# A two-layer decoder trunk on one core: one subtraction, four products and one load change their engine

## Chip, core and metric

The kernel runs on one core of a Trainium2 chip. A core has five engines that run at the same time, each with its own queue of instructions, taken in order: TensorE (PE, matrix products), VectorE (DVE), ScalarE (ACT, functions by table, and copies), GpSimd (POOL) and SyncE (SP, which here only issues transfers). ScalarE can issue transfers as well. Transfers themselves are done by 16 DMA engines that all queues share. The metric is device microseconds for one execution of the whole program, the median of several runs.

## What is computed

The reference is a decoder trunk of two layers on 256 tokens of 1024 features, in float32. Layer 0 mixes tokens by a gated spatial unit (gMLP), layer 1 by an mLSTM; each layer then has a SwiGLU channel mixer and a gated embedding. The parts that the change touches are the first product of layer 0 and the mLSTM's cell and output:

```python
def gmlp_mixer(x, w_in, ...):
    z = jax.nn.gelu(x @ w_in)
    u, v = jnp.split(z, 2, axis=-1)
    ...

def mlstm_cell(q, k, v, i_pre, f_pre):          # 4 heads of 512, chunks of 128
    ...
        s = jnp.einsum('bhtd,bhsd->bhts', qb, kb) * jnp.exp(dmat - m_t[..., None])
        num = (jnp.einsum('bhts,bhsd->bhtd', s, vb) + ...)
        h = num / jnp.maximum(jnp.abs(den), jnp.exp(-m_t))[..., None]

def mlstm_mixer(x, ...):
    h = mlstm_cell(split_heads(q), split_heads(k), split_heads(v), i_pre, f_pre)
    h = layer_norm(h, norm_g).reshape(B, S, ML_INNER) + skip * xc
    return (h * jax.nn.silu(z)) @ w_out
```

With 256 tokens in two chunks the kernel forms the cell's chunks in closed form: for each head a matrix P of scores times decay (the text calls it P), then P·V, then a division and a normalisation per head.

## The kernel before

**Precision by two parts.** A float32 operand is kept as two float32r tiles: the high part is a rounded copy, the low part the difference. Three matmuls (high·high, low·high, high·low) replace one. The helper `split` (lines 151 to 153) makes both: the copy on ScalarE (`act.copy`), the subtraction on VectorE, or on the engine named in `sub`. Every weight tile of 128 x 1024 that arrives goes through it once, so line 153 is the line of nearly all copies and subtractions in the profile; they are told apart by tile names (`w` weights, `xs` x, `phi`/`plo` the two parts of P, `h` the down projection's input).

**Who sets the order.** The instructions of an engine are ordered by a planner that simulates the program with costs of its own and takes what is ready; the text of the kernel gives priorities. Inside `manual_schedule` (line 372 for ScalarE and VectorE at the start, line 859 for ScalarE during the gates) the order is that of the text. All weights come in the order of `weight_plan` through `ahead` (lines 170 to 204), which issues loads on SyncE's queue up to 8 tiles ahead and splits up to 4 tiles ahead; only 4 raw tiles exist, so a load waits for the subtraction that frees a raw tile.

**The start (lines 353 to 390).** TensorE runs eight warm-up matmuls on zeros. x comes transposed in four loads `xr[0..3]` of two 128-row blocks each. `xr[0]` is split in two: its first block is issued by ScalarE (line 363), its second by SyncE through the hook `second_x` (line 364), which `ahead` calls between the two halves of the first weight tile (lines 175 to 178). The first tiles come in halves of 512 columns. Lines 374 to 385 then split x's blocks and the weight halves in an order written by hand: for each block ScalarE copies the block's high part (L378), VectorE or ScalarE copies the weight half's (L380 or L382), and VectorE makes the low parts (L383, L384). TensorE's first matmuls are those of line 422, six for each block.

**The gates and P (lines 859 to 923).** For each of the four heads VectorE adds a mask (L909, tile `gm`), ScalarE takes three exponentials (L911 to L913, tile `e`), VectorE multiplies the scores by them (L917, tile `sc`), and `split` makes `phi` on ScalarE and `plo` on GpSimd (L920).

**P·V and the normalisation (`pv_block`, lines 930 to 967).** For each head TensorE multiplies `phi` and `plo` with V into two PSUM banks `num` (L937 to L939) and sums P's rows into `pd` (L943, L944). VectorE forms the denominator (L949 to L953), the statistics of `num` (L957, L958) and a variance (L961); GpSimd takes the reciprocal root (L962); VectorE finishes scale and shift (L963, L965); ScalarE writes the normalised head `hn` (L967), which frees the two banks. Between two heads TensorE has a block of z (`z_mm`).

**The down projection's input (`h_block`, lines 971 to 983).** For each head TensorE transposes `hn` (L976), VectorE applies the norm's gain and adds the skip (L980, tile `y`), multiplies with silu(z) (L981, tile `sz`), and `split` makes the two parts of `h`. Head 0's `h_block` is called after the third head's `pv_block` and z block, the other heads' during the down projection (`acc`, lines 992 to 1008), whose four PSUM banks are the ones that `num` used. The first three blocks of the projection are held until all are there, and added together (lines 1001 to 1006).

Of the kernel before, what the change touches and what calls it, by code (L numbers as in the profile page):

```python
# [12 lines left out]
ALU = mybir.AluOpType  # L13
# [51 lines left out]
def stationary(key):  # L65

    return key[0] in ("u", "xm") and len(key) == 2 or key[0] in ("g", "u", "z") and key[-1] >= 4


def paired(key):  # L70

    return key[0] in ("g", "u") and len(key) == 3 and key[-1] >= 4 or key[0] == "u" and len(key) == 2
# [61 lines left out]
def trunk(ctx, tc, a, out):  # L134
    nc = tc.nc
    pe, act, dve, pool, sp = nc.tensor, nc.scalar, nc.vector, nc.gpsimd, nc.sync
# [8 lines left out]
    def tl(tag, shape, dt=F32, name="t"):  # L145
        return sb.tile(shape, dt, tag=tag, name=name, bufs=BUFS[tag])
# [4 lines left out]
    def split(hi, lo, src, fast=False, sub=dve):  # L151

        return dve.tensor_copy(hi, src) if fast else act.copy(hi, src), sub.tensor_tensor(lo, src, hi.bitcast(F32), ALU.subtract)  # L153
# [7 lines left out]
    def issue_after(ops):  # L161

        stack = ExitStack()
        for op in ops:
            stack.enter_context(tc.issue_after(op.ins))
        return stack

    at = {"load": 0, "cast": 0, "use": 0}

    def ahead(loads, casts):  # L170
        while at["load"] < min(len(plan), at["use"] + loads):
            ap = plan[at["load"]][1]
            n = ap.shape[-1]
            t = tl("raw", [P, n], name="raw")
            for c in HALF if at["load"] < 3 else [slice(0, n)]:
                at["dma"] = sp.dma_start(t[:, c], ap[:, c])
                if at["load"] == 0 and c.start == 0:
                    second_x()
            raws[at["load"]] = t
            at["load"] += 1  # L180
        while at["cast"] < min(len(plan), at["use"] + casts):
            i = at["cast"]
            key, raw = plan[i][0], raws.pop(i)
            n = raw.shape[-1]
            if key in WIDE:
                t = tl("b8", [P, 2, D], F32R, "w")
            else:


                first = ASIDE if stationary(key) and not paired(key) else 0  # L190
                step = D + ASIDE if paired(key) else D
                t = tl("w", [P, 2 * D + P], F32R, "w")[:, first:first + 2 * step]
                t = t.rearrange("p (i n) -> p i n", i=2)[:, :, :D]
            with issue_after(behind["cast"]):
                if key[0] == "bdv":

                    t = t.rearrange("p i n -> p (i n)")[:, :4 * 2 * GW].rearrange("p (j i n) -> p j i n", j=4, i=2)
                    split(t[:, :, 0, :P], t[:, :, 1, :P], raw.rearrange("p (j n) -> p j n", j=4))
                    f = 4 * key[1]
                    pool.tensor_copy(t[:, :, :, P:], wx[:, f:f + 4, :].rearrange("p j (i n) -> p j i n", i=2))  # L200
                for c in () if key[0] == "bdv" else HALF if i < 3 else [slice(0, n)]:
                    split(t[:, 0, c], t[:, 1, c], raw[:, c])
            wt[i] = t
            at["cast"] += 1
# [153 lines left out]
    xr = []  # L358
    for i in range(4):
        t = tl("m2", [P, 2, S], name="xr")  # L360
        if i == 0:

            act.dma_start(t[:, 0, :], a["xT"][i, :, 0, :])
            second_x = lambda: sp.dma_start(xr[0][:, 1, :], a["xT"][0, :, 1, :])
            xr.append(t)
        else:
            sp.dma_start(t, a["xT"][i])
            xr.append(t)
        ahead(1 + i, 0)
    make_identity(nc, ident)  # L370
    pool.memset(mhalf, -0.5)
    with tc.manual_schedule(engines={mybir.EngineType.Activation, mybir.EngineType.DVE}):

        for i in range(2):
            w, raw = tl("w", [P, 2 * D + P], F32R, "w")[:, :2 * D].rearrange("p (i n) -> p i n", i=2), raws.pop(i)
            for k, h in enumerate(HALF):
                c = 2 * i + k
# [9 lines left out]
    for i in range(2, 4):  # L387
        c = slice(2 * i, 2 * i + 2)
# [4 lines left out]
    for c in range(6):  # L393
# [20 lines left out]
        for kp in range(4):  # L414
            w = weight("v", c, kp)
            for kk in range(2):
                k = 2 * kp + kk
# [284 lines left out]
    def mlstm(embed1):  # L702
# [32 lines left out]
        sz = [tl("b8", [P, 8, S], name="sz") for _ in range(2)]  # L735
# [97 lines left out]
        for s in range(NI + 3):  # L833
            if s < NI:
                y = xm_block(s)
# [23 lines left out]
        with tc.manual_schedule(engines={mybir.EngineType.Activation}):  # L859
            gp = bank("A", [4, 2, S], "gp")  # L860

            def transpose_gates():
                for i in range(2):
                    for t in range(2):
                        pe.transpose(gp[:, i, TOK[t]], gacc[:, t, 4 * i:4 * i + 4], ident)


            tc.keep_in_program_order(act.preload_act_table_set("natural_log_exp_and_others"))
            z8 = z_mm(8, {3: transpose_gates})
            dve.tensor_scalar(fs, gp[:, 1, :], gbias[:, 1:2], None, ALU.add)  # L870
            dve.scalar_tensor_tensor(ex, fs, -1.0, fs, ALU.mult, ALU.min)
            act.activation(ex, ex, AF.Exp)
            act.activation(ex, ex, AF.Ln, bias=1.0)
            dve.scalar_tensor_tensor(fs, fs, 0.0, ex, ALU.min, ALU.subtract)
            dve.tensor_tensor_scan(ex, line, fs, 0.0, ALU.mult, ALU.add)
            dve.scalar_tensor_tensor(ai, gp[:, 0, :], gbias[:, 0:1], ex, ALU.add, ALU.subtract)
            dve.tensor_tensor_scan(G, ai, ai, 0.0, ALU.max, ALU.max)
            dve.tensor_tensor(ex, ex, G, ALU.add)
            Gs = [tl("s", [4, S], F32R, "G") for _ in range(2)]
            behind["cast"] = split(*Gs, G, fast=True)[1:]  # L880
            z_copy(*z8)
            z_copy(*z_mm(9))
            cp = bank("A", [P, 4, 4], "cp")

            def transpose_cols():
                for i, src in enumerate((ai, ex)):
                    for t in range(2):
                        pe.transpose(cp[:, 2 * i + t, :], src[:, TOK[t]], ident[:4, :4])

            gbs = []  # L890

            def broadcast_gates():

                gbs.extend(bank("A", [P, 2, 2, P], "gb") for _ in range(2))
                for h in range(NH):
                    for i in range(2):
                        pe.matmul(gbs[h // 2][:, h % 2], selH[:, h, :], Gs[i], start=i == 0, stop=i == 1)

            z = z_mm(10, {2: transpose_cols, 4: broadcast_gates})
            dve.tensor_copy(cols[:, 0:2, :], cp[:, 0:2, :])  # L900

            dve.tensor_scalar(cols[:, 2:4, :], cp[:, 2:4, :], -88.0, None, ALU.max)
            for h in range(NH):
                if h == 1:
                    z_copy(*z)
                    z = z_mm(11)
                gb = gbs[h // 2][:, h % 2]
                gm = tl("s", [P, 2, P], name="gm")
                dve.tensor_tensor(gm, gb, cmask.unsqueeze(1).to_broadcast([P, 2, P]), ALU.add)  # L909
                e = tl("m2", [P, 384], name="e")  # L910
                act.activation(e[:, 0:P], gm[:, 0, :], AF.Exp, bias=cols[:, 0, h:h + 1], scale=-1.0)  # L911
                act.activation(e[:, P:S], gb[:, 1, :], AF.Exp, bias=cols[:, 0, h:h + 1], scale=-1.0)
                act.activation(e[:, S:384], gm[:, 1, :], AF.Exp, bias=cols[:, 1, h:h + 1], scale=-1.0)  # L913
                if h == 1:
                    act.activation(cols[:, 2:4, :], cols[:, 2:4, :], AF.Exp, scale=-1.0)
                p = sc[h]
                dve.scalar_tensor_tensor(p, p, DH ** -0.5, e, ALU.mult, ALU.mult)  # L917
                hi = tl("h", [P, 384], F32R, "phi")
                lo = tl("h", [P, 384], F32R, "plo")
                split(hi, lo, p, sub=pool)  # L920
                ph.append((hi, lo))
            z_copy(*z)
            act.activation(sz[1][:, 0:4, :], sz[1][:, 0:4, :], AF.Silu)
# [47 lines left out]
        def h_block(h):  # L971
            for j in range(2):
                tp = bank("B", [P, 2, S], "tp")
                for i in range(2):
                    for t in range(2):
                        pe.transpose(tp[:, i, TOK[t]], hn[h][:, t, (2 * j + i) * P:(2 * j + i + 1) * P], ident)  # L976
                for i in range(2):
                    f = 4 * h + 2 * j + i
                    y = tl("s", [P, S], name="y")
                    dve.scalar_tensor_tensor(y, tp[:, i, :], par[:, f, 6:7], a1[f // 8][:, f % 8, :], ALU.mult, ALU.add)  # L980
                    dve.tensor_tensor(y, y, sz[f // 8][:, f % 8, :], ALU.mult)  # L981
                    hs[f] = tl("h", [P, 2, S], F32R, "h")
                    split(hs[f][:, 0, :], hs[f][:, 1, :], y)

# [119 lines left out]
```

## Time and profile before

| What | Value |
|---|---|
| median of 3 runs | 825.69 us (825.42 to 826.16) |
| profiled execution's own time | 825.63 us |
| its span in the profile | 823.9 us |
| data read from HBM | 153.67 MB, 188 GB/s over the span |
| granted TensorE clock | 1.0 throughout |

The profile shows one execution. A row of a timeline gives the start and the duration in us, the engine, the line, the operation, the output tile, the input tiles and their shapes, and in brackets the time for which the engine was idle before it and what ended that idleness. "PEld" is TensorE's loading of stationary operands, which overlaps its matmuls. In the list of waits a row reads: the engine and line that waited, the one that released it, then total us, number of waits, and the longest. Several instructions of a kind can be merged into one row with a count (x2, x3); its duration is then that of all of them. Rows that name line 153 and a tile group a helper's instructions by what they work on. In a row of a window stand its start and end, its length, the busy time and count of each engine, the granted clock, the mean busy share of the 16 DMA engines, and GB/s.

### The profile page before, as it was taken

The numbers are of one execution on the slowest core, as the hardware profiler recorded it, in microseconds if no ns is written. First come the engines' busy times: TensorE is split into PE (matmuls) and PEld (weight loads), VectorE is DVE, ScalarE is ACT, GpSimd is POOL, SyncE is SP. The second block draws the span as 40 slices with busy tenths as digits, with TensorE's granted clock in tenths as the row PEclk, the third lists the DMA queues.
The fourth block names the chain that finished last, engine by engine and source line by source line (L and its number), as shares of the span: only waits on it lengthen the run. The fifth ranks groups of instructions, "written<-read, shape, count | busy, mean of one in ns | idle before, by whom it ended". The sixth has DMA issues, their size and how long they took to land.

```text
span 823.9 us, 12407 instructions
## 1 busy us (share of the span) xinstructions
PE 816.9 (99%) x4520; PEld 708.0 (86%) x4520; DVE 614.3 (75%) x982; ACT 470.9 (57%) x820; POOL 149.6 (18%) x209
## 2 busy tenths in 40 slices
PE   9999999999999999999999999999999999999997
PEld 6888888888888888888889999988888888888886
DVE  6757998678956567586878998889885656776674
ACT  6656666565535556475256788776444555665522
POOL 1020643342000000700001677330000000000000
PEclk9999999999999999999999999999999999999999
DMA  8895447567176678677144355454626667886501
GB/s 287 283 337 182 153 159 225 179 194 243 67 260 202 192 225 281 201 229 252 38 146 156 135 162 161 146 177 147 215 90 224 196 199 228 269 264 212 179 1 51
DMA packets 44997, 155.52 MB, mean 189 GB/s; under 512 B 5256, under 2 KB 6024, under 8 KB 44936
## 3 DMA queue, kind: packets, MB, share of 16 engines
q1 hardware_dynamic: 44792, 154.60, 57.6%
q8 instruction: 35, 0.57, 0.3%
q14 instruction: 26, 0.21, 0.1%
q10 hardware_dynamic: 144, 0.13, 0.0%
HBM read 153.67 MB, written 1.05 MB: 188 GB/s over the span
## 4 chain that ended last, share of the span: by engine, by line
PE 96%; DVE 1%; ACT 1%; DMA 1%; issue 0%; POOL 0%; SPq 0%; DVEq 0%; ACTq 0%
PE acc L240 9%; PE acc L241 9%; PE acc L242 9%; PE pu L260 8%; PE pg L260 8%; PE ups L260 5%; PE pg L264 4%; PE pu L264 4%; PE ups L264 3%; PE vps L242 2%; PE vps L240 2%; PE vps L241 2%; PE xmps L245 2%; PE xmps L247 2%; PE xmps L246 2%; PE gate L289 2%
## 5 line engine op out<-in xcount | busy, mean ns | idle before, releaser
L153 DVE TENSOR_TENSOR w<-raw,w 128x1024 fp32r<-128x1024 f32 (+1 forms) x275 | 333.2, 1219 | 74.7 <-ACT w L153 73.1
L153 ACT CAST w<-raw 128x1024 fp32r<-128x1024 f32 (+1 forms) x275 | 284.9, 1046 | 120.6 <-PE acc L242 25.7
L240 PE MATMUL acc<-w,h 128*128 128x512 f32 x336 | 133.0, 396 | 0.2 <-ACT hn L967 0.2
L241 PE MATMUL acc<-w,h 128*128 128x512 f32 x336 | 131.3, 391 | 0.0
L242 PE MATMUL acc<-w,h 128*128 128x512 f32 x336 | 131.0, 390 | 0.0
L242 PEld LDWEIGHTS acc<-w,h 128*128 128x128 f32 x336 | 63.1, 188 | 13.9
L240 PEld LDWEIGHTS acc<-w,h 128*128 128x128 f32 x336 | 63.1, 188 | 12.1 <-ACT hn L967 0.6
L241 PEld LDWEIGHTS acc<-w,h 128*128 128x128 f32 x336 | 63.1, 188 | 11.2 <-DVE h L153 0.2
L260 PE MATMUL pg<-xs,w 128*128 128x512 f32 x288 | 71.6, 391 | 0.0
L260 PE MATMUL pu<-xs,w 128*128 128x512 f32 x288 | 71.5, 390 | 0.0
L260 PEld LDWEIGHTS pg<-xs,w 128*128 128x128 f32 x288 | 53.8, 188 | 11.0
L260 PEld LDWEIGHTS pu<-xs,w 128*128 128x128 f32 x288 | 53.8, 188 | 11.0
L319 POOL TENSOR_TENSOR rs<-ve,mhalf 128x1 f32<-128x1 f32 x8 | 7.6, 956 | 295.9 <-DVE ve L318 291.3
L271 ACT COPY s<-pg 128x256 f32<-128x256 f32 x36 | 13.4, 372 | 69.7 <-PE pg L264 69.7
L260 PE MATMUL ups<-xs,w 128*128 128x512 f32 x192 | 47.9, 391 | 0.0
L272 DVE TENSOR_TENSOR s<-s,pg 128x256 f32<-128x256 f32 x36 | 15.1, 421 | 42.8 <-ACT s L271 42.7
L260 PEld LDWEIGHTS ups<-xs,w 128*128 128x128 f32 x192 | 35.7, 188 | 7.2
L264 PEld LDWEIGHTS pg<-xs,w 128*128 128x128 f32 x288 | 38.9, 188 | 3.1
L264 PE MATMUL pg<-xs,w 128*128 128x256 f32 x288 | 39.5, 280 | 0.0
L264 PE MATMUL pu<-xs,w 128*128 128x256 f32 x288 | 39.4, 279 | 0.0
L264 PEld LDWEIGHTS pu<-xs,w 128*128 128x128 f32 x288 | 36.5, 188 | 0.3
L245 PE MATMUL xmps<-xs,w 128*128 128x256 f32 x128 | 36.3, 284 | 0.0
(252 smaller groups left out, 1635.7 us busy)
## 6 DMA issues: line engine op xcount, KB each, us to landing
raw<-in_ffn_g SPq DMA_DIRECT2D x44, 512.0 KB, 4.4
raw<-in_ffn_u SPq DMA_DIRECT2D x44, 512.0 KB, 4.6
raw<-in_ffn_d SPq DMA_DIRECT2D x44, 512.0 KB, 4.3
raw<-in_gm_u SPq DMA_DIRECT2D x24, 512.0 KB, 3.5
raw<-in_gm_wo SPq DMA_DIRECT2D x24, 512.0 KB, 3.4
raw<-in_gm_v SPq DMA_DIRECT2D x21, 512.0 KB, 5.2
raw<-in_ple_gate SPq DMA_DIRECT2D x16, 512.0 KB, 4.5
raw<-in_ml_z SPq DMA_DIRECT2D x16, 512.0 KB, 3.8
```

Source lines behind the costliest of these rows:

```text
L153: return dve.tensor_copy(hi, src) if fast else act.copy(hi, src), sub.tensor_tensor(lo, src, hi.bitcast(F32), ALU.subtract)
L240: pe.matmul(ps, lh, w[:, 0, c], start=start, stop=False)
L241: pe.matmul(ps, ll, w[:, 0, c], start=False, stop=False)
L242: pe.matmul(ps, lh, w[:, 1, c], start=False, stop=stop)
L245: pe.matmul(ps, w[:, 0, c], h, start=start, stop=False)
L246: pe.matmul(ps, w[:, 0, c], l, start=False, stop=False)
L247: pe.matmul(ps, w[:, 1, c], h, start=False, stop=stop)
L260: pe.matmul(ps, w[:, 0, k * P:(k + 1) * P], xs[:, k], start=k == 0, stop=False)
L264: pe.matmul(ps[:, 0], w[:, 1, k * P:(k + 1) * P], xh[:, k, :], start=False, stop=k == KD - 1)
L271: act.copy(o, ps[:, 1])
L272: dve.tensor_tensor(o, o, ps[:, 0], ALU.add)
L289: pe.matmul(ps, xl[:, k, TOK[t]], w[:, 0, c], start=False, stop=k == KD - 1)
```

## The change

Three places change. x's second block is issued by ScalarE right behind the first, and the hook between the halves of the first weight tile goes. The low part of P of head 0 is subtracted on VectorE; the other three heads' stay on GpSimd. The four products of head 0 with silu(z) go from VectorE to GpSimd; the other heads' stay on VectorE. What is computed is the same.

```diff
             for c in HALF if at["load"] < 3 else [slice(0, n)]:
                 at["dma"] = sp.dma_start(t[:, c], ap[:, c])
-                if at["load"] == 0 and c.start == 0:
-                    second_x()
...
         if i == 0:
-
-            act.dma_start(t[:, 0, :], a["xT"][i, :, 0, :])
-            second_x = lambda: sp.dma_start(xr[0][:, 1, :], a["xT"][0, :, 1, :])
+            for k in range(2):
+                act.dma_start(t[:, k, :], a["xT"][i, :, k, :])
             xr.append(t)
...
                 lo = tl("h", [P, 384], F32R, "plo")
-                split(hi, lo, p, sub=pool)
+
+                split(hi, lo, p, sub=pool if h else dve)
...
                     dve.scalar_tensor_tensor(y, tp[:, i, :], par[:, f, 6:7], a1[f // 8][:, f % 8, :], ALU.mult, ALU.add)
-                    dve.tensor_tensor(y, y, sz[f // 8][:, f % 8, :], ALU.mult)
+
+                    (dve if h else pool).tensor_tensor(y, y, sz[f // 8][:, f % 8, :], ALU.mult)
```

## The prediction

> **What bounds the kernel now.** I read the page first (busy shares), then TensorE's own waits, then the timelines around each wait.
>
> ```profile
> PE 816.9 (99%) x4520; PEld 708.0 (86%) x4520; DVE 614.3 (75%) x982; ACT 470.9 (57%) x820; POOL 149.6 (18%) x209
> ...
> PE warm L357 <- DVE warm L354: 1.2, 1, 1.2
> PE vps L422 <- ACT w L382: 0.6, 1, 0.6
> PE num L939 <- POOL plo L153: 0.5, 1, 0.5
> PE vps L422 <- ACT xs L378: 0.2, 1, 0.2
> PE acc L240 <- ACT hn L967: 0.2, 1, 0.2
> ...
> 818.46 1.12 PE L289 MATMUL gate<-w,xs 128*128 128x256 f32 x8
> ```
>
> The reader is to see that TensorE is busy for 816.9 of the 823.9 us span, and that the idle 7.0 us are almost listed: 1.2 before the first warm-up matmul, 0.2 + 0.6 in the first product of the kernel, 0.5 in the mLSTM's first P·V, 0.2 at the start of the down projection, and the tail after the last matmul (818.46 + 1.12 = 819.58, to 823.9: 4.3). The change takes no matmul away, so it can win only what stands in these waits. It touches three of them: 0.6, 0.5 and 0.2.
>
> **Part 1: x's second block on ScalarE's queue.** The chain of waits at the start:
>
> ```profile
> 1.24 0.42 SPq L364
> ...
> 1.71 4.98 DMA raw<-in_gm_v
> 6.72 0.63 ACT w L382
> ...
> 7.39 4.38 PE vps L422 x18
> ```
>
> ```profile
> 0.79 0.40 ACTq L363 DMA_DIRECT2D xr<-in_xT  x1
> ...
> 4.57 0.71 ACT L378 CAST xs<-xr 128x256 fp32r<-128x256 f32 x2 [2.06 <-DMA xr<-in_xT]
> ...
> 7.39 0.50 PE L422 MATMUL vps<-w,xs 128*128 128x512 f32 x1 [0.57 <-ACT w L382]
> ...
> 8.09 0.43 DVE L380 CAST w<-raw 128x512 fp32r<-128x512 f32 x1
> ...
> xr<-in_xT SPq DMA_DIRECT2D x1, 128.0 KB, 3.6
> ...
> 0.00:5.00 5.00, 3.60 (x8) 1.04 (x8) 0.93 (x3) 1.72 (x3) 2.57 (x14) 1.00 0.53 165
> 5.00:10.00 5.00, 4.41 (x17) 3.07 (x18) 3.97 (x9) 2.84 (x6) 0.00 (x0) 1.00 1.03 358
> ```
>
> SyncE's queue issues the first weight half, x's second block (1.24), then the second weight half (1.71). That half lands at 1.71 + 4.98 = 6.69, ScalarE casts it (0.63), and TensorE, which had finished the first block's six matmuls, has stood for 0.57. With the block on ScalarE's queue every later issue on SyncE moves up by 1.71 - 1.24 = 0.47. On ScalarE the second issue costs some 0.4 (the first one's duration) at a time when the engine next does something useful at 4.57, after an idle 2.06 behind its table load, so the issue is hidden; were that cover gone it would cost 0.4.
>
> What the earlier issue is worth is bounded: at best the whole 0.57, at worst nothing if transfers and not issues set the landing: the DMA share (next to last column of the two window rows) is 0.53 over the first 5 us, which holds the idle first two, and 1.03 over the next five, with the same bytes to move. Below nothing is rival C. Between these there is a second stop: the next block's weight is cast at 8.09 + 0.43 = 8.52, and it is used after six of the 18 matmuls (4.38 / 18 = 0.243 each), at 7.39 + 1.46 = 8.85. If that half lands no earlier, TensorE can move up by only 0.33. I take **-0.3**, the value with this nearest row behind it, and keep 0 and -0.57.
>
> **Part 2: head 0's low part on VectorE.** Around the 0.47 us stall:
>
> ```profile
> 533.81 0.74 DVE L909 TENSOR_TENSOR gm<-gb,cmask 128x256 f32<-128x256 f32 x2
> ...
> 533.91 0.51 ACT L153 CAST phi<-sc 128x384 fp32r<-128x384 f32 x1 [0.65 <-DVE sc L917]
> ...
> 534.47 1.20 DVE L153 TENSOR_TENSOR w<-raw,w 128x1024 fp32r<-128x1024 f32 x1
> ...
> 534.50 2.04 POOL L153 TENSOR_TENSOR plo<-sc,phi 128x384 fp32r<-128x384 f32 x1 [11.40 <-ACT phi L153]
> ...
> 535.60 1.36 DVE L917 SCALAR_TENSOR_TENSOR sc<-sc,e 128x384 f32<-128x384 f32 x1
> ...
> 536.60 0.50 PE L939 MATMUL num<-vn,plo 128*128 128x512 f32 x1 [0.47 <-POOL plo L153]
> ...
> 542.51 1.02 POOL L153 TENSOR_TENSOR plo<-sc,phi 128x384 fp32r<-128x384 f32 x1 [1.04 <-ACT phi L153]
> ...
> L153 DVE TENSOR_TENSOR xs<-xr,xs x2: 682/684/685, 10.3 to 12.1; 128x512 fp32r<-128x512 f32 x2
> ...
> L383 DVE TENSOR_TENSOR xs<-xr,xs x4: 419/420/426, 5.0 to 9.4; 128x256 fp32r<-128x256 f32 x4
> ```
>
> GpSimd began at 534.50 while VectorE was in a weight's low part to 535.67, and ended at 536.54; alone (542.51) the same subtraction takes 1.02. VectorE's next two-input instruction, which began at 535.60, took 1.36 and ended at 536.96. So the two engines take turns: each waited for the other's end. On VectorE the subtraction lies between the 0.42 of 256 columns and the 0.68 of 512: about 0.55. It can start when ScalarE's high part is there (534.42). VectorE is free at about 534.5, so it ends near 535.05 ahead of the 1.20 weight part, or near 536.2 behind it. TensorE wants it at 536.60 - 0.47 = 536.13. Ahead, the whole **-0.47** comes; behind, about -0.4. If VectorE waits for the high part before the next head's mask (L909 at 533.81), its 0.6 of waiting falls on heads 1 to 3, whose low parts are used one gate product and more later. The order on VectorE is a planner's, so either is possible; both are gains. In return VectorE's 1.36 shrinks towards 0.5, which pays for the added 0.55.
>
> **Part 3: head 0's products on GpSimd, and what is late next.** TensorE arriving 0.47 earlier meets the last of the waits, the bank that the fourth head's numerator leaves:
>
> ```profile
> 555.00 0.76 DVE L981 TENSOR_TENSOR y<-y,sz 128x256 f32<-128x256 f32 x2
> ...
> 553.74 0.69 POOL L962 TENSOR_TENSOR hrs<-hrs,mhalf 128x2 f32<-128x2 f32 x1 [5.60 <-DVE hrs L961]
> ...
> 556.46 1.01 ACT L153 CAST h<-y 128x256 fp32r<-128x256 f32 x3
> ...
> 558.25 0.15 DVE L949 SCALAR_TENSOR_TENSOR dn<-pd,cols 128x2 f32<-128x2 f32 x1
> ...
> 558.32 1.21 DVE L153 TENSOR_TENSOR w<-raw,w 128x1024 fp32r<-128x1024 f32 x1
> ...
> 560.15 0.48 PE L240 MATMUL acc<-w,h 128*128 128x512 f32 x1
> ...
> 560.92 1.29 DVE L957 BATCH_NORM_STATS2 hst<-num 128x6 f32<-128x512 f32 x2
> ...
> 564.51 1.45 ACT L967 ACTIVATE hn<-num,nb,hrs 128x512 f32<-128x512 f32 x2 [0.75 <-DVE nb L965]
> ...
> 565.35 0.50 PE L240 MATMUL acc<-w,h 128*128 128x512 f32 x1 [0.18 <-ACT hn L967]
> ...
> 556.33 0.25 PE L944 MATMUL pd<-ones_r,plo 128*128 128x2 f32 x1
> ...
> L153 POOL TENSOR_TENSOR vn<-vsum,vn 128x256 fp32r<-128x256 f32 x2 | 1.5, 740 | 0.3 <-ACT vn L153 0.2 <-ACT gsum L825 0.2
> ```
>
> TensorE finished the fourth head at 556.33 + 0.25 = 556.58, but VectorE took its denominators up only at 558.25 and its statistics at 560.92, and ScalarE normalised at 564.51. That chain is late because VectorE is full, not because TensorE is. If nothing else changed, the 0.47 would be lost here: the stall of 0.18 would read 0.65. The four products take 0.38 each on VectorE (0.76 for two), so moving them frees 1.5 us ahead of 558.25. That is more than the 0.65 needed, which is why I let both go: **-0.18** more.
>
> The products themselves cost 0.74 each on GpSimd, by its nearest row (also two inputs, 256 columns; the ends are VectorE's own 0.38 and the 1.02 of 384 columns); four take 3.0, from 554.4 when GpSimd ends the root of L962 to 557.4, or about 559 with waits for VectorE. Queued behind each on ScalarE is its cast of h, and behind that VectorE's low part. ScalarE was taking those casts from 556.46 only, after head 2's normalisation, and TensorE reads the first of them at 560.15 and the next ones 1.36 (six matmuls of 0.227) apart; a cover of 2 us or more. If it is gone, TensorE waits for the products directly. GpSimd's next duty, head 3's root near 563, is far behind.
>
> [...]
>
> **Sum**, on the profiled execution's own time of 825.63 (span 823.9 and 1.73 around it; the median of the three runs is 0.06 higher): -0.3 - 0.47 - 0.18 = -0.95, so 824.7.
>
> **Rivals.**
> A. *GpSimd's turns cost VectorE more than the products did.* All four turns on the chain: 4 x 0.74 = 2.96 locked, less 1.5 saved, and the fourth head's normalisation comes up to 1.44 later. The 0.47 goes into that wait and TensorE resumes at 565.35 + 1.44. With -0.3 from the start: +1.14, 826.8, slower than before. It decides from the point where VectorE loses more than 1.5 us to GpSimd's turns. For it: the 1.36 row, and a VectorE that is full here. [...] 0.08.
> B. *The stall only moves.* The products' results come late in VectorE's order, its low parts of h wait, and the denominators start where they did: 0.47 is lost at the bank, only -0.3 stays: 825.3. For it: the denominators stand behind three low parts in the timeline. 0.13.
> C. *x's second block lands late.* It lands at 1.24 + 3.6 = 4.84 now, and ScalarE casts it ahead of the weight half in an order written by hand. If it comes only with the half, at 6.69, the half's cast is 0.36 later (0.71 for two casts); this begins to cost past 6.36. +0.36 - 0.47 - 0.18 = -0.29: 825.3. Against: 1.5 us of room. 0.08.
> [...]
> D. *The first part does nothing*, transfers being the limit: -0.65, 825.0. For it: the share of 1.03. 0.17.
>
> **How the numbers follow.** Forecast 824.7: 0.50; A 0.08; B 0.13; C 0.08; D 0.17; 0.04 for an order of the planner that none of this covers. Best sum -0.57 - 0.47 - 0.18 = -1.22 gives 824.4; the runs lie 0.27 below and 0.47 above their median. The range 824.2 to 826.0 takes in all but A and the last. About 0.2% (1.65 us) is what a measurement of this kernel can tell from no change; below 824.04 nothing in the touched waits reaches, above 827.34 not even A. Faster 0.04, same 0.92, slower 0.04.
>
> **What would show it.** Right: the wait of TensorE on plo is gone from its list, the first head's plo stands on VectorE within 0.5 to 0.6 us, the wait on hn is gone, and the wait on L382 has shrunk to about 0.3. Part 1 is wrong if the weight half still lands at 6.7; C shows as the cast of x's second block starting after 6.3. B shows as a wait on hn of 0.6; A as one above 0.65, with two-input VectorE instructions near 1 us between 554 and 560. The forecast as a whole fails if TensorE shows a wait at a place not listed above.

## The result, and the profile after

| | before | changed |
|---|---|---|
| median, 11 executions each | 825.66 us (825.19 to 826.16) | 828.17 us (826.96 to 830.48) |
| ratio | | 1.0035, 95% interval 1.0027 to 1.0043 |
| profiled execution's own time | 825.63 us | 829.92 us |
| its span | 823.9 us | 828.2 us |

The forecast was 824.7. The kernel became 2.5 us slower. TensorE's list of waits in the profile of the changed kernel (lines here are two or three lower than before: L238 is the old L240, L965 the old L967, L935 the old L937):

```profile
PE acc L238 <- ACT hn L965: 2.2, 1, 2.2
...
PE num L935 <- ACT e L909: 1.0, 1, 1.0
PE vps L419 <- DVE w L377: 0.6, 1, 0.6
```

The wait for `plo` is gone, as intended. The wait for `hn` has grown from 0.2 to 2.2, and a wait of 1.0 stands where there was none. The page's first part says that this is not all:

```profile
PE 818.8 (99%) x4520; PEld 709.2 (86%) x4520; DVE 615.1 (74%) x979; ACT 470.8 (57%) x820; POOL 152.9 (18%) x212
```

TensorE has the same 4520 matmuls, and is idle for 828.2 - 818.8 = 9.4 us, 2.4 more than before; but it is also busy for 1.9 us longer than the 816.9 of before. Together that is the 4.3 by which this execution is longer. The 1.9 are a clock. The timeline of TensorE behind its longest wait:

```profile
567.34 0.50 PE L238 MATMUL acc<-w,h 128*128 128x512 f32 x1 [2.19 <-ACT hn L965]
567.67 0.57 PE L239 MATMUL acc<-w,h 128*128 128x512 f32 x1
...
570.60 0.63 PE L240 MATMUL acc<-w,h 128*128 128x512 f32 x1
...
571.31 0.39 PE L239 MATMUL acc<-w,h 128*128 128x512 f32 x1
```

and that stretch as a window (the clock is the third number from the end):

```profile
567.67:571.08 3.41, 3.41 (x10) 2.66 (x9) 3.11 (x8) 2.42 (x5) 0.00 (x0) 0.51 0.00 0
```

For 3.41 us the granted clock was half, and matmuls started every 0.43 us instead of every 0.23. The cost is about 3.41 x (1 - 0.51) = 1.7 us. Not every execution has it: of the eleven, five show a mean clock of 0.997 to 0.998 and took 829.23 to 830.48 (mean 829.68), six show 0.999 or 1.0 and took 826.96 to 828.17 (mean 827.63). So some 2.0 us of the loss are there always, and another 2.0 in about half of the executions.

**Where the waits come from.** First ScalarE before the change, around head 1's high part (`phi` at 537.00):

```profile
535.59 1.05 ACT L153 CAST w<-raw 128x1024 fp32r<-128x1024 f32 x1
537.00 0.51 ACT L153 CAST phi<-sc 128x384 fp32r<-128x384 f32 x1 [0.36 <-DVE sc L917]
...
538.27 1.03 ACT L153 CAST w<-raw 128x1024 fp32r<-128x1024 f32 x1
...
540.15 0.35 ACT L912 ACTIVATE e<-gb,cols 128x128 f32<-128x128 f32 x1
```

and then the same engine after it:

```profile
535.66 1.05 ACT L153 CAST w<-raw 128x1024 fp32r<-128x1024 f32 x1 [0.16 <-DMA raw<-in_ml_wo]
538.29 1.05 ACT L153 CAST w<-raw 128x1024 fp32r<-128x1024 f32 x1 [1.58 <-DMA raw<-in_ml_wo]
539.24 0.51 ACT L153 CAST phi<-sc 128x384 fp32r<-128x384 f32 x1
...
542.65 0.35 ACT L909 ACTIVATE e<-gb,cols 128x128 f32<-128x128 f32 x1
...
566.51 1.45 ACT L965 ACTIVATE hn<-num,nb,hrs 128x512 f32<-128x512 f32 x2 [0.86 <-DVE nb L963]
```

The reader is to see that the second cast of an output-projection weight now stands ahead of head 1's `phi`. ScalarE takes its instructions in order, the weight's load had not landed, and the engine stood for 1.58 us and then cast for 1.05 while head 1's `phi`, whose scores VectorE had finished at 535.93 + 0.55 = 536.48 (its rows stand below), lay behind it. `phi` came at 539.24 instead of 537.00, and ScalarE's work on the gates and `phi` of heads 2 and 3 followed 2.2 to 3.0 us later. Head 3's exponential that reads the broadcast gates (`e<-gb`) ended at 543.00 instead of 540.50; TensorE wanted that PSUM bank for head 1's second numerator, which is the new wait:

```profile
543.05 0.50 PE L935 MATMUL num<-vn,phi 128*128 128x512 f32 x1 [1.01 <-ACT e L909]
```

VectorE's side of it:

```profile
534.33 0.54 DVE L153 TENSOR_TENSOR plo<-sc,phi 128x384 fp32r<-128x384 f32 x1
...
535.93 0.55 DVE L914 SCALAR_TENSOR_TENSOR sc<-sc,e 128x384 f32<-128x384 f32 x1
...
540.63 1.26 DVE L914 SCALAR_TENSOR_TENSOR sc<-sc,e 128x384 f32<-128x384 f32 x1
...
542.15 0.14 DVE L947 SCALAR_TENSOR_TENSOR dn<-pd,cols 128x2 f32<-128x2 f32 x1
...
562.15 0.15 DVE L947 SCALAR_TENSOR_TENSOR dn<-pd,cols 128x2 f32<-128x2 f32 x1
```

The first row is the change doing what it says, 0.54 us at 534.33. But head 0's denominators stand behind head 2's scores in VectorE's order and came at 542.15 (539.31 before), and the last head's at 562.15 (558.25 before). ScalarE normalised the last head from 566.51 instead of 564.51, and the bank's wait grew by those 2.0.

A second order changed with it, that of TensorE. Its fourth head ended at 557.00 + 0.25 = 557.25 here:

```profile
557.00 0.25 PE L942 MATMUL pd<-ones_r,plo 128*128 128x2 f32 x1
```

Counted from there, TensorE came to the bank after 567.34 - 2.19 - 557.25 = 7.90 us; before, after 565.35 - 0.18 - 556.58 = 8.59. Its timelines show why: between the fourth head and the bank stand the same block of z and the same eight transposes, but 18 matmuls of the down projection instead of 21. So of the 2.0, some 1.3 are the later normalisation (9.26 us behind the fourth head instead of 7.93) and 0.7 are three matmuls that the planner no longer put in front.

### The profile page after: what moved, and what is told of

It reads as the page before. It is cut to its first block, busy times and chain, and to the rows that moved or that the text cites. A ratio compares the mean times of both kernels' runs of the same rounds, so it can differ in the third digit from the quotient of the medians.

```text
span 828.2 us, 12406 instructions
## 1 busy us (share of the span) xinstructions
PE 818.8 (99%) x4520; PEld 709.2 (86%) x4520; DVE 615.1 (74%) x979; ACT 470.8 (57%) x820; POOL 152.9 (18%) x212
## 3 DMA queue, kind: packets, MB, share of 16 engines
HBM read 153.67 MB, written 1.05 MB: 187 GB/s over the span
## 4 chain that ended last, share of the span: by engine, by line
PE 93%; DVE 3%; DMA 1%; ACT 1%; issue 1%; POOL 0%; SPq 0%; DVEq 0%; ACTq 0%; POOLq 0%
PE acc L238 9%; PE acc L239 9%; PE acc L240 9%; PE pu L258 8%; PE pg L258 8%; PE ups L258 5%; PE pg L262 4%; PE pu L262 4%; PE ups L262 3%; PE vps L240 2%; PE vps L238 2%; PE vps L239 2%; PE xmps L243 2%; PE xmps L245 2%; PE xmps L244 2%; PE gate L287 2%
## 5 line engine op out<-in xcount | busy, mean ns | idle before, releaser
L238 PE MATMUL acc<-w,h 128*128 128x512 f32 x336 | 133.5, 397 | 2.2 <-ACT hn L965 2.2
L240 PE MATMUL acc<-w,h 128*128 128x512 f32 x336 | 131.7, 392 | 0.0
L238 PEld LDWEIGHTS acc<-w,h 128*128 128x128 f32 x336 | 63.5, 189 | 14.2 <-ACT hn L965 2.6
L240 PEld LDWEIGHTS acc<-w,h 128*128 128x128 f32 x336 | 63.5, 189 | 13.9
```

Of the source, the lines that this page charges most:

```text
L238: pe.matmul(ps, lh, w[:, 0, c], start=start, stop=False)
L240: pe.matmul(ps, lh, w[:, 1, c], start=False, stop=stop)
```

## The experiments

Three theories. **S**: the order of ScalarE's casts, which the planner changed when the subtraction moved, is the loss. The rival **G**: GpSimd's products and its turns with VectorE are the loss (rival A of the prediction). **C**, beside either: a TensorE wait of about 2 us costs more than its length, by the half clock. Kernels that one paragraph compares ran on one chip and share the runs of the kernel before.

**Each part alone.** x's second block alone (the first two hunks of the change):

> Only x's second block moves to ScalarE's queue; P's low part and the products stay. Both theories of the loss (S: ScalarE's order around head 1's high part of P; G: GpSimd's turns with head 0's products) leave this part out: the start wins 0.3 us, as it does between the profiles of before and after (the k = 4 block's first matmul at 11.61 and 11.31), and TensorE's waits of 0.5 on plo and 0.2 on hn stay: 825.3, clock 1.0. If more than 1 us is lost here, both are wrong and the planner's changed order behind the start is the cause.

Measured 825.0 us (824.62 to 825.52) against 825.36 before, ratio 0.9996 (0.9987 to 1.0005). The sign is not certain from the ratio, but the size is that of the forecast. In its profile no wait on `vps` is left; a single profile says little here, since that of the kernel with four extra writes below, whose start is that of before, has none either.

The low part alone:

```diff
-                split(hi, lo, p, sub=pool)
+                split(hi, lo, p, sub=pool if h else dve)
```

> Only head 0's low part of P on VectorE. S: the planner puts two weight casts, not one, ahead of head 1's high part on ScalarE, and the second waits for its load; high part near 539.2 instead of 537.0, TensorE waits about 1 us for it in the second head's P.V and 1 to 2 us for the fourth head's normalisation: 827 to 829. G: the products are on VectorE, so nothing is lost; the 0.5 stall goes: 825.2.

Measured 827.85 us (827.45 to 830.37, five executions), ratio 1.0037 (1.0024 to 1.0049). Its waits, without any product on GpSimd:

```profile
PE acc L240 <- ACT hn L967: 2.1, 1, 2.1
...
PE num L937 <- ACT e L912: 1.0, 1, 1.0
```

and its ScalarE:

```profile
538.94 1.05 ACT L153 CAST w<-raw 128x1024 fp32r<-128x1024 f32 x1 [1.59 <-DMA raw<-in_ml_wo]
539.89 0.51 ACT L153 CAST phi<-sc 128x384 fp32r<-128x384 f32 x1
```

Both waits, the cast ahead of `phi`, and two executions of five at a clock of 0.997 are there. This one line loses as much as the whole change; G is out as the main cause.

The products alone:

```diff
-                    dve.tensor_tensor(y, y, sz[f // 8][:, f % 8, :], ALU.mult)
+                    (dve if h else pool).tensor_tensor(y, y, sz[f // 8][:, f % 8, :], ALU.mult)
```

> Only head 0's four products on GpSimd. S: ScalarE's order around P is that of before, so no wait in P.V is added; the wait on plo stays at 0.5, that on hn lies between 0 and 0.7: 825.5 to 826.2. G: four products of 1.0 us, with VectorE's low parts of h stretched, put the fourth head's normalisation some 1.5 us later: wait on hn of 1.5 to 2, 827 to 829.

Measured 825.79 us (825.28 to 826.08), ratio 1.0004 (0.9996 to 1.0013): about 0.4 lost, not resolved from none. The `hn` wait is 0.6. Its VectorE:

```profile
553.54 0.68 DVE L963 TENSOR_TENSOR hrs<-hrs,dn 128x2 f32<-128x2 f32 x1 [0.41 <-POOL hrs L962]
...
555.01 0.77 DVE L153 TENSOR_TENSOR h<-y,h 128x256 fp32r<-128x256 f32 x1
555.70 0.47 DVE L980 SCALAR_TENSOR_TENSOR y<-tp,par,a 128x256 f32<-128x256 f32 x1
556.09 1.37 DVE L153 TENSOR_TENSOR w<-raw,w 128x1024 fp32r<-128x1024 f32 x1
557.38 1.63 DVE L153 TENSOR_TENSOR h<-y,h 128x256 fp32r<-128x256 f32 x3
558.93 0.15 DVE L949 SCALAR_TENSOR_TENSOR dn<-pd,cols 128x2 f32<-128x2 f32 x1
```

and its GpSimd:

```profile
553.47 0.74 POOL L981 TENSOR_TENSOR y<-y,sz 128x256 f32<-128x256 f32 x1
554.76 3.29 POOL L981 TENSOR_TENSOR y<-y,sz 128x256 f32<-128x256 f32 x3 [0.55 <-DVE nb L965]
```

The products cost 0.74 each when free and 1.1 with turns. VectorE pays for them: its four low parts of h take 0.77 + 1.63 = 2.40 instead of the 1.10 + 0.42 of before, the multiplication of L963, which also has two inputs, 0.68 instead of 0.16, and the weight part 1.37 instead of 1.21. That is 0.88 + 0.52 + 0.16 = 1.56, all of the 1.5 that was freed.

The longer wait is not explained by this. The rows of TensorE and ScalarE around the bank:

```profile
555.41 0.25 PE L944 MATMUL pd<-ones_r,plo 128*128 128x2 f32 x1
...
563.29 1.45 ACT L967 ACTIVATE hn<-num,nb,hrs 128x512 f32<-128x512 f32 x2 [0.86 <-DVE nb L965]
...
564.12 0.50 PE L240 MATMUL acc<-w,h 128*128 128x512 f32 x1 [0.55 <-ACT hn L967]
```

This execution is ahead of that of the kernel before, so the times are counted from the end of the fourth head, 555.66 here and 556.58 before. The normalisation came 7.63 us behind it instead of 7.93, so it was 0.3 earlier, although the denominators stood later in VectorE's order. But TensorE came to the bank after 7.91 us instead of 8.59, again with 18 matmuls of the down projection in front instead of 21. By these rows the wait grew because of TensorE's order and not because of GpSimd's turns. No run has the products with TensorE's old order.

**The order put back.** The low part on VectorE as above, and in addition the second weight's cast held behind head 1's `phi`:

```diff
-            with issue_after(behind["cast"]):
+            with issue_after(tuple(behind["cast"]) + (behind["phi", 1] if key == ("mo", 1) else ())):
...
-                split(hi, lo, p, sub=pool)
+                behind["phi", h] = split(hi, lo, p, sub=pool if h else dve)[:1]
```

> Head 0's low part on VectorE, and one edge more: the cast of the second output-projection weight is issued on ScalarE behind head 1's high part of P, as it was before. S: head 1's high part is back near 537, no wait in P.V, the 0.5 wait on plo gone; the wait on hn between 0.2 and 0.7 since TensorE comes earlier: 825.2 to 825.7, clock 1.0. G: the same as e2 (825.2). If the loss of e2 stays here although the high part is on time, the order of that cast isn't its cause.

Measured 825.92 us (825.15 to 826.49), ratio 1.0005 (0.9996 to 1.0014), every clock 0.999 or 1.0. ScalarE's rows are back where they were:

```profile
536.19 0.51 ACT L153 CAST phi<-sc 128x384 fp32r<-128x384 f32 x1
...
537.58 1.05 ACT L153 CAST w<-raw 128x1024 fp32r<-128x1024 f32 x1
```

One edge between two instructions of one engine takes back 1.9 us of the 2.5 that the low part had cost, a little less than expected (825.2 to 825.7). This shows S for the larger part of the loss. TensorE has its 21 matmuls ahead of the bank again, so the planner's order on TensorE went back with that on ScalarE. What is left has another place, again in ScalarE's order; its rows a little later:

```profile
545.23 0.78 ACT L967 ACTIVATE hn<-num,nb,hrs 128x512 f32<-128x512 f32 x1 [2.71 <-DVE nb L965]
545.90 1.05 ACT L923 ACTIVATE sz<-sz 128x1024 f32<-128x1024 f32 x1
546.85 0.77 ACT L967 ACTIVATE hn<-num,nb,hrs 128x512 f32<-128x512 f32 x1
```

The planner now puts the large Silu (1.05) between head 0's two normalisations, and TensorE shows 0.6 for `hn` at a numerator. VectorE's multiplication that feeds this normalisation took 0.96 instead of the 0.16 of before; in the changed kernel the same one took 0.97 (at 546.57) beside GpSimd's next `plo` (546.50 to 547.52).

**Parts 1 and 2, then all three, with the order kept.** Besides the edge above, a third weight's cast is held behind head 0's normalisation, and the normalisations behind the Silu:

```diff
+            with issue_after((*behind["cast"], *behind.get({("mo", 1): ("phi", 1), ("mo", 2): "hn"}.get(key), ()))):
...
+            behind["silu"] = [act.activation(sz[1][:, 0:4, :], sz[1][:, 0:4, :], AF.Silu)]
...
+                with issue_after(behind["silu"]): behind[h == 0 and "hn"] = [act.activation(o[:, t, :], num[t], AF.Identity, bias=nb[:, t:t + 1], scale=rs[:, t:t + 1])]
```

The first of the two kernels has x on ScalarE's queue and the low part on VectorE, without the products:

> x's second block on ScalarE's queue and head 0's low part on VectorE; the second output-projection weight's cast behind head 1's high part, the third's behind head 0's normalised head, and the normalised heads behind the large Silu, so that ScalarE's order is nearly that of before. S: no wait on plo, none above 0.3 on the banks of heads 1 to 3, except the last (hn), which may read up to 0.65 since TensorE comes 0.47 earlier: 824.6 to 825.1, below x alone (825.0) or equal to it. If a wait of 0.5 or more stands at a bank again, VectorE's chain from head to head is the limit and the low part's 0.47 is never won.

Measured 825.24 us (824.81 to 825.52) against 825.52, ratio 0.9998 (0.9989 to 1.0006), a little above the 825.1 expected at most. Besides the one at the warm-up, one wait is left in TensorE's list:

```profile
PE acc L240 <- ACT hn L967: 0.7, 1, 0.7
```

The starting wait and the one for `plo` are both gone from the list, but the bank's has grown from 0.2 to 0.7. The second gain is given back at the last head's bank, as part 3 said it would be without relief.

The second kernel is the whole change with those edges:

> The whole change, with the same three edges on ScalarE. S: the loss of the change (2.5) is the order of the casts, so this returns to 825 to 825.6; what is above the run without the products is GpSimd's turns (0.4 in the products' own run). G: the loss stays, 827 to 828, with a wait of 1.5 or more on hn.

Measured 825.85 us (825.26 to 826.22), ratio 1.0003 (0.9994 to 1.0012), all clocks 0.999 or 1.0, and

```profile
PE acc L240 <- ACT hn L967: 1.3, 1, 1.3
```

That is 0.25 above the range of S and well below that of G. So with the order kept the change costs nothing that can be told from no change, instead of 2.5 us. With the products the bank's wait is 0.6 longer (1.3 against 0.7) and the median 0.6 higher. Counted from the end of the fourth head, the normalisation comes after 8.37 us with the products and after 8.48 without, so they relieve the chain by 0.1 only; TensorE comes after 7.90 instead of 8.60, since the three matmuls are missing in front of the bank here too. The three edges hold ScalarE's order, not TensorE's.

**A wait of a chosen length.** To test C, head 3's first normalisation was written again and again (the same values), which delays the bank by 0.67 each time. Nothing of the result changes.

```diff
-            for t in range(2):
+            for t in [0] * 2 * (h == NH - 1) + [0, 1]:
```

> The kernel before, with the fourth head's first normalisation written three times instead of once (the same values again), so that TensorE's bank comes two copies of 0.73 later. Theory C (TensorE standing idle for long draws its clock down for 3.4 us): a wait of about 1.6 on hn, time +1.4 (826.8), granted clock still 1.0 in all windows. Without C: the same time.

Measured 825.59 us against 825.52, ratio 0.9999. With four extra writes instead of two:

> The same with four copies more: a wait of about 3.1 on hn. Without C: +2.9 (828.3) and a granted clock of 1.0 between 560 and 580. With C: in most executions a stretch of 3.4 us at half clock behind the wait, 1.7 more: about 830, mean clock 0.997.

Measured 825.6 us, ratio 1.0001. Both missed, because no wait arose. The list of waits with four extra writes:

```profile
PE acc L240 <- ACT hn L967: 0.2, 1, 0.2
```

The planner gave TensorE other matmuls (24 of the down projection instead of 21) and the other bank first: TensorE went on at 565.32, while ScalarE wrote until 567.92 + 0.78 = 568.70. A lateness that stands in the program costs nothing here; that the one in the changed kernel hurt because the planner did not see it coming is likely, but no run shows the planner's own times. So TensorE's order was pinned for the first four blocks of the down projection, before repeating this with one, two and four extra writes:

```diff
+        keep = tc.keep_in_program_order if pinned else lambda i: i
+        keep(pe.matmul(ps, lh, w[:, 0, c], start=start, stop=False)), keep(pe.matmul(ps, ll, w[:, 0, c], start=False, stop=False))
+        keep(pe.matmul(ps, lh, w[:, 1, c], start=False, stop=stop))
...
-                mm_tok(self.ps[t][j], h[:, 0, TOK[t]], h[:, 1, TOK[t]], w, HALF[j], f == 0, f == self.n - 1)
+                mm_tok(self.ps[t][j], h[:, 0, TOK[t]], h[:, 1, TOK[t]], w, HALF[j], f == 0, f == self.n - 1, self.n == NI and f < 4)
```

> The kernel before, with TensorE's matmuls of the first four down-projection blocks held in the order of the text, so that the last head's bank is added in behind 18 of them whatever the planner thinks, and with head 3's first hn written once more than needed (0.74 us). The wait for hn should be about 1.6 us (0.2 + 0.7 + 0.7). Theory that a long wait of TensorE itself costs more than its length, by a stretch at half clock: at 1.6 us not yet, 825.5 + 1.4 = 826.9, clock 1.0. Theory that waits cost only their length: the same 826.9. If the half clock comes at this length already: 828.5 in some executions.

Measured 826.02 us (825.56 to 826.33) against 825.29, clocks 0.999 or 1.0. The wait was 0.64, not 1.6.

> As the run before, with the hn written twice more: a wait for hn of about 2.3 us, as long as the 2.2 us that the changed kernel shows. If a wait costs only its length: 825.5 + 2.1 = 827.6 in every execution, clock 1.0. If a wait of this length draws a stretch at half clock behind it in a share of the executions: two groups, near 827.6 at clock 1.0 and near 829.5 at 0.997 to 0.998.

Measured 826.67 us (826.06 to 826.95), all eleven executions at 0.999 or 1.0. There were two waits, not one:

```profile
565.88 0.74 PE L241 MATMUL acc<-w,h 128*128 128x512 f32 x2 [0.64 <-ACT hn L967]
...
567.52 0.73 PE L241 MATMUL acc<-w,h 128*128 128x512 f32 x2 [0.67 <-ACT hn L967]
```

> As before, with the hn written four times more: a wait for hn of about 3.8 us. Length only: 825.5 + 3.6 = 829.1, clock 1.0. With the stretch at half clock, now in nearly every execution: 830.8 to 831, clock 0.997.

Measured 828.69, 830.49, 831.16 and 831.39 us, with mean clocks 1.0, 0.997, 0.995 and 0.995. The profiled execution (830.49) has a wait of 0.64 and one of 2.45, and then:

```profile
569.51 0.73 PE L241 MATMUL acc<-w,h 128*128 128x512 f32 x2 [2.45 <-ACT hn L967]
...
571.96 0.63 PE L242 MATMUL acc<-w,h 128*128 128x512 f32 x1
...
574.42 0.40 PE L242 MATMUL acc<-w,h 128*128 128x512 f32 x1
```

The doses came out smaller than expected, since the planner put eight transposes (1.04 us) in front, and the wait fell into one for each of the two banks; so these runs do not give a threshold. Nor does a run have TensorE pinned and nothing else. They do show C: two waits of 0.64 and 0.67 drew no slow stretch in eleven executions, one of 2.45 drew it in three of four. By lengths alone the last kernel would be at 826.67 + (0.64 + 2.45 - 0.64 - 0.67) = 828.45, which is near the execution with the full clock; the other three lie 2.0 to 2.9 above it. The two at a mean clock of 0.995 lost more than one such stretch takes; neither is profiled, so why stays open. With the low part and the products as in the kernel before, a TensorE wait of 2.45 us brought the slow stretch of the changed kernel in three executions of four.

**One block more ahead of the bank.** The kernel with parts 1 and 2 and the order kept, TensorE pinned as above, and four down-projection blocks instead of three ahead of the last head's bank:

```diff
-                if f < 3:
+                if f < 4:
...
-                    for t in range(2) if f == 2 else ():
+                    for t in range(2) if f == 3 else ():
```

> Parts 1 and 2 of the change with the order of ScalarE's casts kept, and 24 matmuls (5.45 us, four blocks) in place of 18 ahead of the last head's bank on TensorE. If what was left of the loss was only that the bank came 0.7 us late for TensorE, the wait for hn is under 0.2 us and the time 825.5 - 0.35 - 0.47 - 0.18 = 824.5, 824.8 at most. If something else takes the gain back: 825.2 as without the fourth block.

Measured 824.78 us (824.28 to 825.04) against 825.29 (824.77 to 825.72), ratio 0.9993 (0.9984 to 1.0002). TensorE's list of waits has only the warm-up's left:

```profile
PE warm L357 <- DVE warm L354: 1.2, 1, 1.2
```

This is the best version, 0.5 us under the kernel before in the medians (0.3 without the fourth block); the interval still touches no change. The time lies in the expected 824.5 to 824.8, but these were worked out from 825.5, as a gain of 0.7 to 1.0, and against the 825.29 of this chip only 0.5 was gained. So giving TensorE other work took the wait at the bank away, which freeing VectorE had not; how much of its 0.7 us came back as time, these runs do not resolve.

## Why the prediction was wrong

**What bounds the kernel: right.** The time moved with TensorE's waits. That was also the limit of the forecast: it summed the waits that stood in the list, took only those on `hn` and at the start as able to grow, and none as able to arise.

**Part 1: the size right, the mechanism not shown.** Alone the part gave 0.36 in the medians, near the 0.3 forecast. The start of the changed kernel on TensorE:

```profile
8.47 3.00 PE L419 MATMUL vps<-w,xs 128*128 128x512 f32 x12 [0.56 <-DVE w L377]
11.31 0.39 PE L238 MATMUL vps<-w,xs 128*128 128x512 f32 x1
```

The 0.57 for the first weight half is gone, and the second stop named in the prediction, the next block's weight, took its place with 0.56. The product behind the 24 matmuls of the start began at 11.31; in the timeline of the kernel before its row is

```profile
11.61 0.39 PE L240 MATMUL vps<-w,xs 128*128 128x512 f32 x1
```

That these two rows differ by the forecast 0.30 is luck. Nine of the profiled kernels have the start of before, and in them this product begins anywhere from 10.78 to 11.85 (mean 11.48); in the five with part 1 from 10.95 to 11.44 (mean 11.19). The means differ by the forecast 0.3, single executions by more. The late weight half from which the prediction reasoned is not the rule either: ScalarE casts it at 6.72 in the kernel before and at 6.91 in the one with two extra writes, but at 5.15 to 5.33 in the other seven with the same start, most of which wait at the second stop instead. With part 1 it is cast at 5.52 to 5.63 in all five. So the gain can't be put down to the earlier issue of that half. Rival C falls: x's second block, on ScalarE in the changed kernel, came ahead of the point of 6.36 from which C decides:

```profile
5.21 0.41 ACT L375 CAST xs<-xr 128x256 fp32r<-128x256 f32 x1 [0.51 <-DMA xr<-in_xT]
```

Rival D, that the part does nothing, is made unlikely by the 0.36, whose interval touches no change.

**Part 2: the step that failed** is "The order on VectorE is a planner's, so either is possible; both are gains." The order on VectorE came out as the first of the two (0.54 at 534.33, the wait on `plo` gone). The orders that mattered were ScalarE's and TensorE's, of which that step says nothing. When the subtraction moved, the planner put the cast of a weight whose load landed late ahead of head 1's `phi`. Waits of 2.0 more at the last bank and 1.0 at the gates' bank, less the 0.47 and the 0.30 that were won, make +2.2; the executions with the full clock lie 827.63 - 825.66 = 2.0 above before. The half clock adds 1.7 to 2 in the others. The forecast gave this 0.04, as "an order of the planner that none of this covers". Its own last sentence, that it fails if TensorE waits at a place not listed, is what happened. That ScalarE's order is the cause of the larger part is shown by the single edge that undoes 1.9 of the 2.5; why the planner preferred it, and when it took the load to land, stays open.

**Part 3: wrong too.** "Moving them frees 1.5 us ahead of 558.25" holds for the products themselves, but the turns with GpSimd take 1.56 back (rows of the products alone). What was left for the last head's normalisation was 0.3 there and 0.1 with the order of the casts kept, instead of the 0.65 needed. And the part took TensorE's arrival at the bank as given, where the planner moved it 0.7 earlier by three matmuls. "A cover of 2 us or more" did not matter. In the changed kernel the four products took 1.0 each, not 0.74:

```profile
557.28 3.99 POOL L980 TENSOR_TENSOR y<-y,sz 128x256 f32<-128x256 f32 x4 [0.86 <-DVE y L978]
```

Rival A had one half of this, the 1.5 us of VectorE lost to turns; its price, a normalisation up to 1.44 later, did not come, and the 0.4 to 0.6 that the products cost are, by the rows above, TensorE's order. Three kinds of VectorE instruction with two inputs stand beside the products, and each took longer there: the first low part of h 0.77 instead of 0.42 at most, a weight's 1.37 instead of 1.21, and L963 0.68 instead of 0.16. A product of L980 between them, which reads PSUM, took 0.47, as before (0.48). Rival B, the stall that only moves, is what the kernel with parts 1 and 2 shows: 0.7 at the bank.

**The sum.** With ScalarE's order kept, the forecast's -0.95 is +0.3 (825.85 against 825.52): about -0.35 at the start, the 0.47 moved to the bank and not won, and 0.6 with the products. The rest of the 2.5, 2.2 us, is the order of the casts with what it draws behind it.

## What to carry to other kernels

Where a planner orders the queues, moving one instruction off an engine is a change to every queue: compare the order of all engines, the one that bounds the kernel too, and above all look for an instruction that waits for a load and now stands ahead of work on the chain, since the engine takes it in order and passes its wait on: here 1.58 us for a load, and `phi` 2.24 us later. A wait that is taken away ahead of a later bound is won only if there is other work to put in front of that bound, as the fourth block was here. Taking instructions from VectorE to GpSimd can cost VectorE as much as it frees: the four products alone freed 1.5 us, and VectorE's low parts and L963 beside them took 1.56 longer. And where a start varies by 1 us from execution to execution, two single profiles can't show a gain of 0.3.

## What was unexpected of the hardware

A TensorE wait of 2.1 to 2.5 us was followed by a stretch at half the granted clock (0.51), 3.41 us long in the changed kernel, starting 0.3 us after the wait there and 1.3 us after it in the pinned kernel with four extra writes (0.51 from 570.80 to 574.30), where a wait of 0.64 stood 1.0 us ahead of the long one. By the mean clock, since one execution of each is profiled, it came in 5 of 11, 2 of 5 and 3 of 4 executions of the three kernels with such a wait, and in none of those with single waits up to 1.3 us (two executions of the products alone show a mean clock of 0.998, at ordinary times). Why only some executions have it, and how long a wait must be for it, these runs do not settle.
